# Seven-product pairs in a down projection, with operand sums and weight differences made earlier and kept in DRAM

## The chip, the cores and the metric

The kernel runs on one core of a Trainium2 chip. TensorE multiplies matrices, VectorE and ScalarE work on tiles in SBUF, GpSimd (POOL) has a few small copies and issues some DMAs, and SyncE (SP) issues nearly all loads. The metric is the device time of one execution, in microseconds.

## The reference

One decoder block on 256 tokens of width 2048, in float32: two token mixers merged into one output projection, a LayerNorm with a scaled residual, a gated MLP, a second LayerNorm, and a per-layer embedding (PLE). The part at issue:

```
def conv_gated_mlp(x, w_gate, w_up, conv_w, conv_b, w_down):
    g = causal_dwconv(x @ w_gate, conv_w, conv_b)      # width 3 along the tokens
    h = jax.nn.gelu(g) * (x @ w_up)                     # 256 x 5632
    return h @ w_down                                   # 256 x 2048

x = layer_norm(ALPHA * x + ffn, ln2_g, ln2_b)
x = x + sigmoid(x @ w_ple_gate) * (p @ w_ple_proj)
```

## The kernel before

**Precision.** Each float32 operand is split in two: a rounded part, "hi", and the remainder, "lo". A product is made of three matmuls: hi by hi, hi by lo, lo by hi. Weights are in DRAM as units (`wu[u]`) of 128 x 2048, 1 MB. A unit is loaded as two raw tiles of 128 x 1024 (512 KB) by the SP queue, into a ring of five buffers; ScalarE copies a tile to its hi (line 110), and VectorE subtracts to get the lo (line 176, or line 149 in a seven-product unit). There are six hi and six lo buffers. `prep()` (line 163) writes these steps for one unit; `unit()` writes them for up to three units ahead of the one that TensorE is given.

**Who orders the work.** The instructions of SP stand in the order in which the program text issues them. The other engines are ordered by a scheduler when the kernel is built, except for TensorE in the LayerNorm tails, which is written out by hand. Each engine then works in its order, and an instruction that waits holds up all behind it on that engine.

**The MLP.** 44 slices n of 128 hidden columns. For each, TensorE makes the gate (`psg`) and the up product (`psu`) from one unit each; VectorE and POOL do the convolution, ScalarE the GELU, and VectorE multiplies by the up part, which gives h of slice n, 128 x 256 (lines 1246 to 1282). The activations h stay in SBUF, in two forms, because of the next part.

**The down projection.** Two halves of 1024 output columns (`down`, line 1302). Each takes the 44 slices as 22 pairs; a pair needs one unit: 256 rows of the weight by 1024 columns. It is a product of 2 x 2 blocks (two token blocks of 128, two rows of the pair, two column blocks of 512). `s_half` (line 731) does a pair in one of two ways:

- classic: eight block products, 24 matmuls of 512 columns, all added in four PSUM banks. The operand is h split in hi and lo, in tiles `hC` (line 1276).
- seven products, as in Strassen's scheme: 21 matmuls. Its left operands are three blocks of h and four sums of blocks, split, in tiles `hS` (line 1270; the sums are made at line 710, on VectorE). Its right operands are three blocks of the weight and four differences of blocks. In `prep_s` (line 136) the differences are made at line 152, in place in the raw tiles, after the blocks themselves have been split; then ScalarE and VectorE split the differences. So such a unit costs VectorE four differences and holds its raw tiles longer.

The products of all the seven-product pairs of a half gather in common PSUM banks, and after the last of them `fold()` (line 771) adds them into the residual z2 by nine operations. At the end of a half `ev` (line 1308) adds the classic sums.

Eight of the 22 pairs are seven-product pairs (`DN_S`, line 55). Of these, four have their sums made in the MLP loop and four (`DN_Y`) after it. The order of the pairs (`DN_ORDER`, line 58) puts classic pairs between and behind them; in both halves the last seven-product pair, 19, is followed by more than two classic ones. Half 1 is called with tail = 2: its last two pairs, 20 and 21, are written into `end2` (line 1320) by token block, mixed with the steps of the second LayerNorm. Loads of the residual (`z2`), of LayerNorm gains and of the PLE weights are issued from within the halves.

Of the kernel before, what the change touches and what calls it, by code (L numbers as in the profile page):

```python
# [19 lines left out]
P = 128  # L20
# [32 lines left out]
WO_C = (0, 2, 4, 6, 7)  # L53


DN_S = (1, 4, 6, 9, 11, 14, 16, 19)
DN_Y = (11, 14, 16, 19)
DN_C = tuple(n for n in range(NF // 2) if n not in DN_S)
DN_ORDER = ((0, 1, 2, 4, 3, 6, 5, 9, 7, 8, 11, 10, 14, 12, 16, 13, 19, 15, 17, 18, 20, 21),
            (0, 1, 2, 4, 3, 6, 5, 9, 7, 11, 8, 14, 10, 16, 12, 19, 13, 15, 17, 18, 20, 21))  # L60
AFF1 = ((0, 2, 3), (0, 2))
AFF2 = ((0, 2), (0, 2))
LN_ORDER = (1, 0, 3, 2)
# [7 lines left out]
def tile_block(ctx: ExitStack, tc: tile.TileContext, wu, wfv, wpp, xT_in, x_in, pT_in, wlr,  # L71
# [22 lines left out]
    def s8(shape, dt=F32, name=None):  # L94
        return big.tile(shape, dt, tag="S8", name=name)
# [4 lines left out]
    def t2(name):  # L100
        return sm.tile([P, 512], F32, tag="t2", bufs=6, name=name)
# [7 lines left out]
    def copy(o, i, scale=1.0):  # L109
        return nc.scalar.activation(o, i, AF.Copy, bias=0.0, scale=scale)  # L110
# [18 lines left out]
               for nh in range(2) for i, n in enumerate(order[nh]) if n in sset[nh]}  # L129
    ready = {}  # L130

    def lo_tile(u, name):
        o = 0 if any(u in r for r in UA) else LO_SHIFT
        return rlo.tile([P, 1152], F32R, tag="lo", name=f"lo{name}")[:, o:o + 1024]

    def prep_s(u):
# [4 lines left out]
        for h, r in enumerate((r0, r1)):  # L141
            nc.sync.dma_start(r, wu[u, :, h * 1024:(h + 1) * 1024])
        b12, b11, b22, b21 = r0[:, 0:512], r0[:, 512:1024], r1[:, 0:512], r1[:, 512:1024]

        def split(src, name, e=slice(0, 1024)):
# [3 lines left out]
            nc.vector.tensor_tensor(lo, src, hi.bitcast(F32), ALU.subtract)  # L149
            return [(hi[:, o:o + 512], lo[:, o:o + 512]) for o in range(0, src.shape[1], 512)]  # L150

        sub = lambda o, a, b: nc.vector.tensor_tensor(o, a, b, ALU.subtract)  # L152
# [547 lines left out]
    def cell(o, i):  # L700

        return o[:, i, 0:P], o[:, i, P:256]
# [522 lines left out]
    hC, hS, hY, yps = {}, {}, [], {}  # L1225

    def gate_up(name):
        if first:
# [6 lines left out]
    for n in range(NF):  # L1235
        psg = gate_up(f"psg{n}")


        g = t2(f"gp{n}")
        nc.gpsimd.memset(g[:, 0:2], 0.0)  # L1240
        comb(psg, g[:, 2:258])
        cw = [chn[:, c_cw + j * NF + n:c_cw + j * NF + n + 1] for j in range(3)]
        for i in range(2):
            nc.gpsimd.tensor_copy(g[:, 258 + i:259 + i], g[:, 129 - i:130 - i])
        y = t1("yc")
        nc.vector.tensor_scalar(y, g[:, 2:258], cw[2], chn[:, c_cb + n:c_cb + n + 1],
                                ALU.mult, ALU.add)
# [8 lines left out]
        pair, j = n // 2, n % 2  # L1256
        if pair in DN_S:
            if j == 0:
                if pair in DN_Y:
                    if not hY:  # L1260
                        hY.append(s8([P, len(DN_Y), 2, 256], name="hY"))
                    yps[pair] = hY[0][:, DN_Y.index(pair)]
                else:
                    yps[pair] = t2("yp").rearrange("p (k t) -> p k t", t=S)
            nc.vector.tensor_tensor(yps[pair][:, j, :], y, u, ALU.mult)
            if j == 1 and pair not in DN_Y:
                hS[pair] = sums(yps.pop(pair), f"hS{pair}")
        else:
            nc.vector.tensor_tensor(y, y, u, ALU.mult)
            i = DN_C.index(pair)  # L1270
            if i % 2 == 0 and j == 0:
                hC[i // 2] = (s8 if i < 12 else late.tile)([P, 4, 512], F32R,
                                                           name=f"hC{i // 2}")
            dst = hC[i // 2][:, i % 2 * 2 + j, :]
            copy(dst[:, 0:256], y)
            nc.vector.tensor_tensor(dst[:, 256:512], y, dst[:, 0:256].bitcast(F32),
                                    ALU.subtract)
        if n >= 4:
            pull(1)

    for pair in DN_Y:
        hS[pair] = sums(yps.pop(pair), f"hS{pair}")


    z2 = [None, None]
# [15 lines left out]

    def down(nh, tail, mid):
        def cl(pair, j, t):
            i = DN_C.index(pair)
            a = hC[i // 2][:, i % 2 * 2 + j, :]
            return a[:, t * P:t * P + P], a[:, 256 + t * P:256 + t * P + P]

        def ev(t, c, ps):
            g = 2 * nh + c
            with tc.high_priority(P_STAT if tail else 0):  # L1310
                nc.vector.tensor_tensor(z2of(t, g), z2of(t, g), ps, ALU.add)
                if tail:
                    bn(t, g)

        s_half("dn", nh, DN_ORDER[nh], DN_S, cl, lambda pair, i: cell(hS[pair], i), z2of, ev,
               tail, mid, end2, 1 if tail else 3)

    turns = []
# [206 lines left out]
```

## Time and profile before

| | |
|---|---|
| median of 3 runs | 1666.52 us (1666.16 to 1666.75) |
| the profiled execution | 1666.29 us, its span 1664.5 us |
| TensorE busy | 1658.4 us of the span |
| VectorE busy | 1264.9 us, 76% |
| ScalarE busy | 884.0 us, 53% |
| moved by DMA | 331 MB, 199 GB/s in the mean |

The span runs from the first instruction to the last; the time of the execution has 1.8 us more around it. In the trace the MLP begins at 842.9 us, in the tail of the first LayerNorm, and ends at 1333, the first half of the down projection between 1333.8 and 1448, and the second between 1448 and 1562. In a row of groups the parts are: the line, the engine, the operation, output and inputs with their sizes, the count, then the busy time and the mean of one in ns, then the idle time of the engine just before them and what ended it. "x" on TensorE's rows counts matmul instructions. Names such as `raw`, `hi`, `lo`, `dn`, `dn_p`, `z` are those of the program's tiles; `dn_p` are the PSUM banks of the seven products, `dn` the banks of the classic sums.

### The profile page before, as it was taken

The numbers are of one execution on the slowest core, as the hardware profiler recorded it, in microseconds if no ns is written. First come the engines' busy times: TensorE is split into PE (matmuls) and PEld (weight loads), VectorE is DVE, ScalarE is ACT, GpSimd is POOL, SyncE is SP. The second block draws the span as 40 slices with busy tenths as digits, with TensorE's granted clock in tenths as the row PEclk, the third lists the DMA queues.
The fourth block names the chain that finished last, engine by engine and source line by source line (L and its number), as shares of the span: only waits on it lengthen the run. The fifth ranks groups of instructions, "written<-read, shape, count | busy, mean of one in ns | idle before, by whom it ended". The sixth has DMA issues, their size and how long they took to land.

```text
span 1664.5 us, 24153 instructions
## 1 busy us (share of the span) xinstructions
PE 1658.4 (100%) x8966; PEld 1440.9 (87%) x8966; DVE 1264.9 (76%) x1895; ACT 884.0 (53%) x1293; POOL 43.1 (3%) x171
## 2 busy tenths in 40 slices
PE   9999999999999999999999999999999999999998
PEld 8988888888888888888898888888888888888887
DVE  7776877888876757778987777766667798888874
ACT  6755555655554654545475455544444565455543
POOL 0000000000000000000010000000000000000000
PEclk9999999999999999999999999999999999999999
DMA  8755455545664555567655665555555556676554
GB/s 321 248 170 170 169 176 175 185 155 199 202 227 172 172 177 191 190 214 257 229 190 191 215 215 190 190 189 191 190 189 190 177 180 225 215 265 236 175 188 155
DMA packets 92007, 331.04 MB, mean 199 GB/s; under 512 B 10296, under 2 KB 11584, under 8 KB 90736
## 3 DMA queue, kind: packets, MB, share of 16 engines
q1 hardware_dynamic: 91104, 325.29, 57.4%
q0 software_dynamic: 784, 4.20, 0.7%
q8 instruction: 70, 1.15, 0.3%
q14 instruction: 49, 0.40, 0.1%
HBM read 324.20 MB, written 5.25 MB: 198 GB/s over the span
## 4 chain that ended last, share of the span: by engine, by line
PE 98%; DMA 0%; DVE 0%; ACT 0%; POOL 0%; issue 0%; SPq 0%; POOLq 0%
PE dn L753 11%; PE psu L243 9%; PE psg L243 9%; PE psm L243 7%; PE pg L289 5%; PE psu L245 5%; PE psg L245 5%; PE wo L753 4%; PE gv L753 4%; PE psm L245 4%; PE psa L243 4%; PE gr L289 3%; PE dn_p L753 3%; PE fv L408 2%; PE gr L753 2%; PE psa L245 2%
## 5 line engine op out<-in xcount | busy, mean ns | idle before, releaser
L176 DVE TENSOR_TENSOR lo<-raw,hi 128x1024 fp32r<-128x1024 f32 x512 | 623.2, 1222 | 298.1 <-ACT hi L110 296.7
L110 ACT ACTIVATE hi<-raw 128x1024 fp32r<-128x1024 f32 x512 | 540.2, 1059 | 507.3 <-issue 232.9
L243 PE MATMUL psu<-x1T,hi 128*128 128x512 f32 x688 | 240.4, 392 | 0.0
L243 PE MATMUL psg<-x1T,hi 128*128 128x512 f32 x672 | 234.8, 392 | 0.0
L245 PE MATMUL psu<-x1T,lo 128*128 128x256 f32 x688 | 192.3, 280 | 0.0
L245 PE MATMUL psg<-x1T,lo 128*128 128x256 f32 x672 | 187.8, 280 | 0.0
L243 PE MATMUL psm<-xT,hi 128*128 128x512 f32 x512 | 181.2, 396 | 0.0
L243 PEld LDWEIGHTS psu<-x1T,hi 128*128 128x128 f32 x688 | 129.1, 188 | 27.6
L243 PEld LDWEIGHTS psg<-x1T,hi 128*128 128x128 f32 x672 | 126.1, 188 | 27.0
L245 PE MATMUL psm<-xT,lo 128*128 128x256 f32 x512 | 143.2, 280 | 0.0
L245 PEld LDWEIGHTS psu<-x1T,lo 128*128 128x128 f32 x688 | 130.7, 190 | 0.0
L245 PEld LDWEIGHTS psg<-x1T,lo 128*128 128x128 f32 x672 | 127.6, 190 | 0.0
L753 PE MATMUL dn<-hi,hC 128*128 128x512 f32 x448 | 123.8, 389 | 0.0
L243 PEld LDWEIGHTS psm<-xT,hi 128*128 128x128 f32 x512 | 96.2, 188 | 19.7
L110 ACT ACTIVATE hi_t<-raw 128x1024 fp32r<-128x1024 f32 x56 | 59.5, 1062 | 84.4 <-DVE raw L152 69.5
L753 PEld LDWEIGHTS dn<-hi,hC 128*128 128x128 f32 x448 | 84.0, 188 | 17.4
L245 PEld LDWEIGHTS psm<-xT,lo 128*128 128x128 f32 x512 | 97.2, 190 | 0.1
L243 PE MATMUL psa<-oT,hi 128*128 128x512 f32 x256 | 89.5, 392 | 0.0
L149 DVE TENSOR_TENSOR lo_t<-raw,hi_t 128x1024 fp32r<-128x1024 f32 x56 | 68.4, 1222 | 5.2 <-ACT hi_t L110 3.6
L245 PE MATMUL psa<-oT,lo 128*128 128x256 f32 x256 | 71.6, 280 | 0.0
L753 PE MATMUL dn<-lo,hC 128*128 128x512 f32 x224 | 70.2, 389 | 0.0
L289 PE MATMUL pg<-hi,x2T 128*128 128x512 f32 (+1 forms) x256 | 69.7, 380 | 0.0
(375 smaller groups left out, 2992.6 us busy)
## 6 DMA issues: line engine op xcount, KB each, us to landing
raw<-in_wu_dram SPq DMA_DIRECT2D x568, 512.0 KB, 4.0
fvraw<-in_wfv_dram SPq DMA_DIRECT2D x13, 524.0 KB, 7.0
lnb<-in_lng_dram SPq DMA_DIRECT2D x4, 1024.0 KB, 9.5
z<-in_x_dram SPq DMA_DIRECT2D x2, 1024.0 KB, 6.8
praw<-in_wpp_dram SPq DMA_DIRECT2D x4, 512.0 KB, 5.0
x1d<-z POOLq DMA_DIRECT2D x2, 1024.0 KB, 6.2
z<-x1d SPq DMA_DIRECT2D x4, 512.0 KB, 7.5
xraw<-in_xT_dram SPq DMA_DIRECT2D x7, 256.0 KB, 6.9
```

The source lines that it names most:

```text
L110: return nc.scalar.activation(o, i, AF.Copy, bias=0.0, scale=scale)
L149: nc.vector.tensor_tensor(lo, src, hi.bitcast(F32), ALU.subtract)
L176: i = nc.vector.tensor_tensor(lo, raw, hi.bitcast(F32), ALU.subtract)
L243: nc.tensor.matmul(ps, lhsT=hi[i // 8 if hoff == 0 else 0][:, w0 % 1024:w0 % 1024 + P], rhs=a[:, kt % 4, :], start=first and i == 0, stop= ...
L245: nc.tensor.matmul(ps[:, 256:512], lhsT=lo[i // 8 if hoff == 0 else 0][:, w0 % 1024:w0 % 1024 + P], rhs=a[:, kt % 4, 0:256], start=False, ...
L289: nc.tensor.matmul(bs[j][:, 0:m], lhsT=x, rhs=v[:, o:o + m], start=first and i == 0, stop=last and i == 2)
L408: nc.tensor.matmul(fbk[t][c][:, 0:n], lhsT=x, rhs=w[:, o:o + n], start=kt == 0 and i == 0, stop=kt == 15 and i == 2)
L753: nc.tensor.matmul(ps, lhsT=x, rhs=w, start=todo[id(ps)] == total[id(ps)], stop=todo[id(ps)] == 1)
```

## The change

- 12 pairs are done by seven products instead of 8, in both halves, and the pairs run in their natural order, 0 to 21.
- The four left sums of such a pair are made in the MLP loop, split there, and stored in DRAM (`sd`, two stores of 256 KB by POOL's queue). In the down projection each seven-product unit loads its 512 KB of sums back by SP (`hS`, now per half and pair). The three operands that are plain blocks come from `hC`, which now holds all 44 slices.
- For 8 of the 12 pairs (`DN_T`), in both halves, so 16 units, the four weight differences are made during the MLP: `park_gen` loads the unit (1 MB, SP), VectorE makes the four differences in it, and POOL's queue stores it in DRAM (`td`, 1 MB). It starts at slice 6, and its steps are spread over the rest of the loop. In the down projection such a unit takes four raw tiles: the half tile b11 and the tile b22/b21 from the weight, and two tiles of differences from `td`. VectorE makes no differences there then.
- `DN_Y` and the sums after the loop are gone.

```diff
-DN_S = (1, 4, 6, 9, 11, 14, 16, 19)
-DN_Y = (11, 14, 16, 19)
...
+DN_ORDER = (tuple(range(NF // 2)),) * 2
+DN_S = (1, 2, 4, 6, 7, 9, 11, 12, 14, 16, 17, 19)
+DN_T = (2, 4, 7, 9, 12, 14, 17, 19)
...
+    parked = {dn0 + nh * (NF // 2) + n: nh * len(DN_T) + i
+              for nh in range(2) for i, n in enumerate(DN_T)}
...
+    def park_gen():
...
+        for u, i in parked.items():
+            w = s8([P, 2048], name=f"td{i}")
+            nc.sync.dma_start(w, wu[u])
+            yield
+            for h in range(2):
+                differences(w[:, 0:1024], w[:, 1024:2048], h)
+            nc.gpsimd.dma_start(td[i], w)
+            yield
...
     def prep_s(u):
...
+        rt = (r0, r1)
+        if u in parked:
+            nc.sync.dma_start(b11, wu[u, :, 512:1024])
+            nc.sync.dma_start(r1, wu[u, :, 1024:2048])
+            rt = [ring.tile([P, 1024], F32, tag="raw", bufs=5, name=f"rawt{u}_{h}")
+                  for h in range(2)]
+            for h, r in enumerate(rt):
+                nc.sync.dma_start(r, td[parked[u], :, h * 1024:(h + 1) * 1024])
+        else:
+            for h, r in enumerate((r0, r1)):
+                nc.sync.dma_start(r, wu[u, :, h * 1024:(h + 1) * 1024])
+        if dn0 <= u < dn0 + NF:
+            nh, pair = (u - dn0) // (NF // 2), (u - dn0) % (NF // 2)
+            hS[nh, pair] = s8([P, 4, 256], F32R, name=f"hS{nh}_{pair}")
+            nc.sync.dma_start(hS[nh, pair].bitcast(F32), sd[DN_S.index(pair)].rearrange(
+                "p (i n) -> p i n", i=4))
...
         x11, = split(b11, "b11", slice(512, 1024))
         x22, x21 = split(r1, "b2")
-        sub(b11, b12, b11)
-        sub(b12, b12, b22)
-        t3, t1_ = split(r0, "t13")
-        sub(b22, b22, b11)
-        sub(b21, b21, b22)
-        t2_, t4 = split(r1, "t24")
+        if u not in parked:
+            differences(r0, r1, 0)
+        t3, t1_ = split(rt[0], "t13")
+        if u not in parked:
+            differences(r0, r1, 1)
+        t2_, t4 = split(rt[1], "t24")
...
+        nc.vector.tensor_tensor(h, y, u, ALU.mult)
+        dst = hC[n // 4][:, n % 4, :]
+        copy(dst[:, 0:256], h)
+        nc.vector.tensor_tensor(dst[:, 256:512], h, dst[:, 0:256].bitcast(F32), ALU.subtract)
+        if pair in DN_S and j == 1:
+            v = s_sums(yp)
+            for i in range(2):
+                w = sm.tile([P, 2, 256], F32R, tag="t2", bufs=6, name="hs")
+                copy(w[:, :, 0:P], v[:, 2 * i:2 * i + 2])
+                nc.vector.tensor_tensor(w[:, :, P:256], v[:, 2 * i:2 * i + 2],
+                                        w[:, :, 0:P].bitcast(F32), ALU.subtract)
+                nc.gpsimd.dma_start(sd[DN_S.index(pair), :, 512 * i:512 * i + 512],
+                                    w.rearrange("p i n -> p (i n)").bitcast(F32))
...
+        def st(pair, i):
+            if i < 3:
+                return cl(pair, (0, 1, 1)[i], (0, 0, 1)[i])
+            return cell(hS[nh, pair], i - 3)
```

More of the change, by code (lines that the diff above doesn't have):

```diff
@@ L130, in tile_block @@
     ready = {}
+    parked = {dn0 + nh * (NF // 2) + n: nh * len(DN_T) + i
+              for nh in range(2) for i, n in enumerate(DN_T)}
+    td = dr.tile([len(parked), P, 2048], F32, name="td")
+    sd = dr.tile([len(DN_S), P, 1024], F32, name="sd")
+    hS = {}
     def lo_tile(u, name):
@@ L134, in lo_tile, with differences @@
         return rlo.tile([P, 1152], F32R, tag="lo", name=f"lo{name}")[:, o:o + 1024]
+    def differences(r0, r1, h):
+        b12, b11, b22, b21 = r0[:, 0:512], r0[:, 512:1024], r1[:, 0:512], r1[:, 512:1024]
+        sub = lambda o, a, b: nc.vector.tensor_tensor(o, a, b, ALU.subtract)
+        if h == 0:
+            sub(b11, b12, b11)
+            sub(b12, b12, b22)
+        else:
+            sub(b22, b22, b11)
+            sub(b21, b21, b22)
+    def park_gen():
[7 more added lines that the diff above has]
+            yield
     def prep_s(u):
@@ L1224, in tile_block @@
     late.tile([P, GAPS[2]], F32, name="gap2")
-    hC, hS, hY, yps = {}, {}, [], {}
+    hC = {}
+    parks = [park_gen()]
+    n0 = 6
     def gate_up(name):
@@ L1256, in tile_block @@
         pair, j = n // 2, n % 2
+        if n % 4 == 0:
+            hC[n // 4] = (s8 if n < 40 else late.tile)([P, 4, 512], F32R, name=f"hC{n // 4}")
         if pair in DN_S:
             if j == 0:
[L1259 to L1264, printed above, removed]
@@ L1265, in tile_block @@
-            nc.vector.tensor_tensor(yps[pair][:, j, :], y, u, ALU.mult)
-            if j == 1 and pair not in DN_Y:
-                hS[pair] = sums(yps.pop(pair), f"hS{pair}")
-        else:
[L1269 to L1277, printed above, removed]
+                yp = t2("yp").rearrange("p (k t) -> p k t", t=S)
@@ new lines, in tile_block @@
+            h = yp[:, j, :]
+        else:
+            h = y
+        nc.vector.tensor_tensor(h, y, u, ALU.mult)
[11 more added lines that the diff above has]
+                                    w.rearrange("p i n -> p (i n)").bitcast(F32))
@@ L1278, in tile_block @@
         if n >= 4:
             pull(1)
-    for pair in DN_Y:
-        hS[pair] = sums(yps.pop(pair), f"hS{pair}")
+        steps = 2 * len(parked)
+        if n >= n0 and (n - n0) * steps // (NF - 3 - n0) != (n - n0 + 1) * steps // (NF - 3 - n0):
+            pull(1, parks)
+    while parks:
+        pull(1, parks)
     z2 = [None, None]
@@ L1313, in ev @@
                     bn(t, g)
-        s_half("dn", nh, DN_ORDER[nh], DN_S, cl, lambda pair, i: cell(hS[pair], i), z2of, ev,
+        s_half("dn", nh, DN_ORDER[nh], DN_S, cl, st, z2of, ev,
                tail, mid, end2, 1 if tail else 3)
```

10 lines of the change are left out of this document (2 added, 8 removed).

## The prediction

> **What bounds the kernel now.** I read the page first, then the chain in order of time through the down projection, the engines' busy time by stage, the groups of instructions, the landing times of the weight tiles, and what the SP queue waits for.
>
> ```profile
> span 1664.5 us, 24153 instructions
> PE 1658.4 (100%) x8966; PEld 1440.9 (87%) x8966; DVE 1264.9 (76%) x1895; ACT 884.0 (53%) x1293; POOL 43.1 (3%) x171
> PEclk9999999999999999999999999999999999999999
> PE 98%; DMA 0%; DVE 0%; ACT 0%; POOL 0%; issue 0%; SPq 0%; POOLq 0%
> PE dn L753 11%; PE psu L243 9%; PE psg L243 9%; PE psm L243 7%; PE pg L289 5%; PE psu L245 5%; PE psg L245 5%; PE wo L753 4%; PE gv L753 4%; PE psm L245 4%; PE psa L243 4%; PE gr L289 3%; PE dn_p L753 3%; PE fv L408 2%; PE gr L753 2%; PE psa L245 2%
> ```
>
> TensorE is busy through the whole span, at the full clock, and 98% of the chain is its own. So a matmul less is a gain in full, and any wait of TensorE, of which there is none now, is a loss in full. The chain through the first down pairs gives the prices:
>
> ```profile
> 1333.83 5.49 PE dn L753 x24
> 1339.32 0.68 PE dn_p L753 x3
> 1340.00 1.36 PE dn L753 x6
> 1341.36 2.04 PE dn_p L753 x9
> 1343.40 6.12 PE dn L753 x27
> ```
>
> Three matmuls of 512 columns take 0.68 us, 0.2267 each. A classic pair has 24 (5.44 us). A seven-product pair has 21: rows two to four and three of the 27, 0.68 + 1.36 + 2.04 + 0.68 = 4.76 us. The stages (columns: stretch, busy us of PE, PEld, DVE, ACT, POOL, granted clock, DMA share, GB/s):
>
> ```profile
> 860.00:1320.00 460.00, 460.00 (x2661) 407.02 (x2661) 329.20 (x497) 229.76 (x333) 24.32 (x129) 1.00 0.58 197
> 1334.00:1448.00 114.00, 114.00 (x505) 94.39 (x504) 98.44 (x117) 60.89 (x68) 0.00 (x0) 1.00 0.63 212
> 1448.00:1562.00 114.00, 114.00 (x505) 94.43 (x504) 97.37 (x114) 60.39 (x65) 1.00 (x1) 1.00 0.68 233
> 1526.00:1548.00 22.00, 22.00 (x99) 18.23 (x98) 20.68 (x24) 14.43 (x16) 0.00 (x0) 1.00 0.82 285
> 1490.00:1500.00 10.00, 10.00 (x46) 8.29 (x45) 7.56 (x9) 5.58 (x6) 0.00 (x0) 1.00 1.00 398
> 20.00:25.00 5.00, 5.00 (x34) 5.00 (x33) 4.30 (x5) 3.63 (x5) 0.00 (x0) 1.00 1.04 415
> ```
>
> The first is the MLP, the next two are the halves of the down projection. There VectorE is 86% busy, the DMA engines carry 212 and 233 GB/s, and TensorE never waits.
>
> **The change, part by part.**
>
> *Matmuls.* Eight pair-halves go from classic to seven products (four pairs, two halves): 8 x 3 = 24 matmuls, the 24 that the built order has fewer on PE. 24 x 0.2267 = 5.44 us off the path. Each half then needs 12 x 4.76 + 10 x 5.44 = 111.5 us of TensorE instead of 114.2.
>
> *VectorE and ScalarE in the MLP.*
>
> ```profile
> L176 DVE TENSOR_TENSOR lo<-raw,hi 128x1024 fp32r<-128x1024 f32 x512 | 623.2, 1222 | 298.1 <-ACT hi L110 296.7
> L110 ACT ACTIVATE hi<-raw 128x1024 fp32r<-128x1024 f32 x512 | 540.2, 1059 | 507.3 <-issue 232.9 <-DMA raw<-in_wu_dram 37.0 <-PE psu L243 36.3
> L152 DVE TENSOR_TENSOR raw<-raw,raw 128x512 f32<-128x512 f32 x56 | 38.5, 688 | 1.1
> L1276 DVE TENSOR_TENSOR hC<-yc,hC 128x256 fp32r<-128x256 f32 x28 | 11.7, 418 | 0.5 <-ACT hC L110 0.5
> L710 DVE TENSOR_TENSOR sums<-yp 128x128 f32<-128x128 f32 x14 | 4.1, 291 | 0.4
> L775 DVE TENSOR_TENSOR fold<-fold,dn_p 128x512 f32<-128x512 f32 x6 | 4.1, 680 | 0.0
> ```
>
> 16 units x 4 differences x 0.69 = 44 us of VectorE come in. Sums and splits: 12 pairs x (4 x 0.291 + 2 x 0.418) = 24.0 and 16 further hC remainders x 0.418 = 6.7, against some 10 (four pairs' sums) inside the loop before: 20 more. The stage goes from 329 of 460 to 393, 85%, less than the 86% at which the down projection runs without a wait. The 10 us of sums after the loop go, at no gain, since TensorE never waited for them. POOL gets 40 DMA issues between its tap copies, at the issue times below 22 us in all, on an engine with 24 of 460.
>
> *DMA in the MLP.* 16 x (1.05 in + 1.05 out) + 12 x 0.52 out = 40 MB in about 455 us, 87 GB/s on 197: 284, below the 398 of the row above.
>
> ```profile
> L1220 POOL DMA_DIRECT2D x1d<-z x2 | 1.1, 540 | 18.1 <-DVE z L1084 18.1
> x1d<-z POOLq DMA_DIRECT2D x2, 1024.0 KB, 6.2
> ```
>
> A 1 MB store took 6.2 us; a parked unit has some 21 us before its tile is needed again. Its load stands in the SP queue ahead of the next raw tiles, and VectorE's first difference can find it 2 us late, which the two to three prepared units hide. Cost 0; without that cover 16 x 2 = 32 us.
>
> *Down projection, loads.* A half has 10 classic pairs (two raw tiles), 4 seven-product pairs as before (two tiles), 8 parked ones (four tiles, the first of half size), and 12 loads of stored sums. Bytes: 14 x 1.05 + 8 x 1.84 + 12 x 0.52 = 35.7 MB; with the two z2 loads 36.7, which is 329 GB/s over 111.5 us; in the second half, with gains and PLE weights, 40.1 MB, 360 GB/s. Before it was 212 and 233. All raw tiles go through a ring of five. A slot is held from issue to landing (L), then through ScalarE's hi and VectorE's lo. The landings, in the two halves, in 1526 to 1548 and in 1490 to 1500:
>
> ```profile
> DMA to landing us min/median/max: 3.5/5.3/10.8
> DMA to landing us min/median/max: 4.6/5.9/7.2
> DMA to landing us min/median/max: 5.7/6.4/6.6
> ```
>
> So L rises with traffic: 5.3 at some 220 GB/s, 5.9 at 285, 6.4 at 398. A plain tile holds its slot for L + 1.06 + 1.22 + about 0.4 of queueing, L + 2.7. A parked unit's four: 4L + 9.7 (the first is half). A unit with differences: about 2L + 13.5 (hi, lo, two differences, lo of the other tile, hi, lo: 6.2; for the second tile 7.3). Half 0 needs 20(L + 2.7) + 8(4L + 9.7) + 4(2L + 13.5) = 60L + 186 slot-us from five slots; half 1 with two PLE tiles 62L + 191. Before it was 44L + 184, 83 us at L 5.3 against 114: that is why nothing waits. After:
> at L 5.3: 101 us against 111.5, no wait; at 5.9: 108, just enough; at 6.4: 114 and 117.6.
> I take 5.9 in half 0 (329 GB/s is nearest the 285 row) and 6.4 in half 1 (360 is nearest the 398 row). Half 1 then runs 6.1 us over. Ends: L 5.3 costs 0, L 7.2 costs 12 and 16 us.
>
> *Stored sums right behind.* In the SP queue a unit's sums stand after its four raw tiles, and the seven products read them third, 1.36 us into the unit. Where a parked unit follows a unit with differences, its fourth raw slot comes free only when that unit's lo t13 is done, and back-to-back raw issues are 1.1 us apart:
>
> ```profile
> 1350.30 1.47 SPq L172 DMA_DIRECT2D raw<-in_wu_dram  x2
> SPq L142 <- DVE lo_t L149: 72.1, 13, 8.5
> ACT hi L110 <- PE dn L753: 13.9, 10, 1.7
> ```
>
> (Two issues of 0.33 us in 1.47; SP's waits for a slot; ScalarE waiting for TensorE to free a hi tile, which shows how far ahead the preparation is.) The sums land 1.1 + 5.9 = 7.0 us after that, and 4.76 - 2.04 + 1.36 = 4.1 us lie between TensorE's own use of t13 and of the sums. So VectorE must be 2.9 us ahead there. In half 0 it starts some 4 ahead and loses about 1 per five pairs: 1 us of waits in the last group. Ends 0 and 5 (four groups, about 1.2 each).
>
> *Order, and the tail.* The last seven-product pair is now pair 19 directly before 20 and 21. In half 1 these two are the tail, so the fold meets it. The built order of VectorE there is: z2 += p1, lo 266_0, fold += p6, lo 266_1, z2 += fold, lo 267_0, z2 += p5, lo 267_1, fold += p7, z2 += dn 00. p6 is complete 0.68 us before the tail starts. From there 0.68 + 1.22 puts lo 266_1 at 1.3 us into the tail, wanted at 0.9; then 0.69 + 1.22 and 0.68 + 1.22 put 267_0 at 3.2 and 267_1 at 5.1, wanted at 1.6 and 2.3. The last is 2.9 us late, and TensorE waits that long. Now VectorE idles there:
>
> ```profile
> 1554.24 0.69 DVE L1311 TENSOR_TENSOR z<-z,dn 128x512 f32<-128x512 f32 x1 [4.85 <-PE dn L753]
> 1562.20 1.53 PE L289 MATMUL pp<-pw,pTs 128*128 128x512 f32 x6
> 1563.56 0.60 PE L1041 MATMUL ptl<-ident,z 128*128 128x128 f32 x4
> ```
>
> The LayerNorm behind it moves by about the same, so nothing is added. Ends 0 (if TensorE had waited before, p6 and the tail move together, so 0 only if the order differed on the chip) and 5. In half 0 the same fold is covered by two classic pairs.
>
> *Sum.* -5.44 + 0 (MLP) + 1 + 6.1 + 2.9 = +4.6 us on the profiled execution's 1666.29 (span 1664.5 and 1.8 around it; 0.2 below the median): 1671 us.
>
> **A rule weighed.** The rows of five and ten microseconds carried 415 and 398 GB/s. The Trainium skill, "DMA: Bandwidth & Descriptors", Specifications, gives a limit of about 358 GB/s for a core's HBM, and says that a core alone may show more. By that limit half 1's 40.1 MB would take 112.0 us, and the sum would be 1666.3 - 5.4 + 0.5 + 2.9 = 1664.3. The two rows disagree with it as a ceiling; no row here shows 100 us at such a rate.
>
> **Rivals.**
> 1. Loads hidden, tail paid: 111.5 us is just enough at L = (557.5 - 186)/60 = 6.2 in half 0 and (557.5 - 191)/62 = 5.9 in half 1, so L is at most 5.9 in both. For it: raw landings of 3.5 when few are in flight, and the sums are extra transfers outside the ring. Against it: 5.9 already at 285 GB/s. 1666.3 - 5.4 + 2.9 = 1663.8. Chance 0.18.
> 2. The whole saving stands: as rival 1, and VectorE reaches the fold so that the tail's tiles are in time, 1660.9, faster. It decides if TensorE waits less than 2 us in all. For it: now there is no wait at VectorE's 86%. Against: the order's dependence on p6. Chance 0.15.
> 3. Both halves are bound by transfers: L 7, (420 + 186)/5 = 121.2 and (434 + 191)/5 = 125, 9.7 and 13.5 over: 1666.3 - 5.4 + 23.2 + 2.9 = 1687. For it: landings up to 10.8 beside the gain loads. Against: as TensorE waits, traffic falls. Chance 0.09.
> 4. The MLP waits: late parked loads hold VectorE, in order, and use up its 67 free us, 4 per unit. Against: the row of 197 GB/s leaves room. Some 5 us on the forecast, 1676. Chance 0.07.
> 5. The transfer engines, not the ring, bound half 1. The stage rows give 212/0.63, 233/0.68 and 285/0.82, 336 to 348 GB/s at a full share. 40.1 MB at 343 take 116.9 us, 5.4 over, the 36.7 MB of half 0 107.0, none: 1666.3 - 5.4 + 5.4 + 2.9 = 1669.2. Against: 398 at share 1.00. Chance 0.04. The rule above is the same with a smaller price.
>
> **How the numbers follow.** Forecast 0.47, its own range 1667 to 1679. About 0.2% (3.3 us) is what a measurement here can tell from no change. Faster: rival 2 and an edge of rival 1, 0.16. Same: rivals 1 and 5 and the lower end of the forecast, 0.28. Slower: the rest, 0.56. The range reaches from rival 2 up to just short of rival 3: 1661 to 1684.
>
> **What would show it.** Right: MLP with TensorE still full and VectorE near 85%; in the down projection TensorE waiting for hS loads and for lo tiles, more in half 1; landings near 6 us; the first matmuls of unit 267 waiting for lo, with some 3 us in the tail. Wrong: no waits in the halves (rival 1), landings at 7 or more (3), waits in psg or psu (4).

## The result and the profile after

The changed kernel took 1689.84 us in the median of four runs (1687.47 to 1690.69), the kernel before 1666.34: 1.0139 times as long, interval 1.0121 to 1.0156. The forecast was 1671 with a range up to 1684. The sign was right, the size was not. The profiled execution, the shortest of the four, has a span of 1685.7 us, 21.2 more than before. Three lines of the changed kernel's page (the span, the engines' busy time, and the shares of the chain of work that ended last), and its stages (columns as in the prediction; stretches: the MLP, half 0, half 1, its tail):

```profile
span 1685.7 us, 24498 instructions
PE 1663.6 (99%) x8942; PEld 1435.6 (85%) x8942; DVE 1299.2 (77%) x1975; ACT 901.4 (53%) x1325; POOL 73.0 (4%) x211
PE 83%; DMA 7%; DVE 6%; issue 2%; ACT 2%; SPq 0%; POOL 0%; POOLq 0%; ACTq 0%; DVEq 0%
```

```profile
860.00:1320.00 460.00, 460.00 (x2662) 407.02 (x2661) 373.11 (x605) 237.38 (x361) 54.23 (x168) 1.00 0.79 283
1334.00:1450.00 116.00, 112.41 (x485) 89.64 (x483) 84.36 (x88) 64.25 (x70) 0.00 (x0) 1.00 0.87 305
1450.00:1568.00 118.00, 108.56 (x452) 84.35 (x451) 88.29 (x94) 63.98 (x69) 0.00 (x0) 0.99 0.89 322
1568.00:1582.00 14.00, 11.91 (x50) 8.90 (x49) 13.18 (x21) 5.47 (x7) 1.00 (x1) 1.00 0.44 164
```

The 24 matmuls are gone (8966 to 8942). In the MLP TensorE is full and VectorE has 373 of 460 us. The time is lost in the down projection, where VectorE fell from 86% to 73 and 75%, and transfers stand on the chain. What TensorE waited for there (us in total, number of waits, the longest):

```profile
PE dn L791 <- ACT hi_t L108: 3.7, 2, 3.3
PE dn_p L791 <- ACT hi_t L108: 3.1, 3, 1.2
PE dn L791 <- DVE lo L214: 2.6, 4, 0.8
PE dn L791 <- DMA hS<-sd: 1.5, 2, 0.9
PE dn_p L791 <- DVE lo_t L188: 1.3, 3, 0.6
PE dn L791 <- DVE lo_b L188: 1.0, 2, 0.6
```

The largest are for `hi_t`, the rounded differences. Below, "waits" are what a stretch takes, from the start of its first matmul to the start of the next stretch, beyond 0.2267 us for each of its matmuls; they take in the slow starts behind a wait. By this count half 0 has 6.6 us, half 1 up to its tail 15.8, and the tail 3.0. With -5.4 for the matmuls the down projection is 19.9 us longer (248.4 against 228.5), and the stage behind it is 1.3 longer: together the 21.2. Some expectations below quote counts that differ from this one; the text gives this one throughout.

Where the waits begin is seen in SP's queue around 1500 us (start, time from the first issue to the end of the last, queue, line, tile, number of issues):

```profile
1498.23 1.33 SPq L177 DMA_DIRECT2D raw<-in_wu_dram  x2
1499.66 0.46 SPq L181 DMA_DIRECT2D hS<-sd  x1
1502.05 0.33 SPq L169 DMA_DIRECT2D raw<-in_wu_dram  x1
1504.70 0.33 SPq L170 DMA_DIRECT2D raw<-in_wu_dram  x1
1505.98 10.07 SPq L174 DMA_DIRECT2D rawt<-td  x2
1516.14 0.38 SPq L181 DMA_DIRECT2D hS<-sd  x1
```

L177 is pair 11, which makes its differences in place; L169 to L174 are the four tiles of pair 12, which is parked. Its last tile is issued ten microseconds behind the third. This is the longest of the eight such places: the in-place unit's own tiles took 11.5 us to land here, behind the two 1 MB gain loads issued at 1497, where the median of half 1 is 6.1. At the other seven the last tile came 1.3 to 8.9 us behind the third. With each tile's issue matched to its landing and to the end of its lo, the trace shows a ring that is full throughout: a slot is taken again 0.03 us after it is free, nearly everywhere. The first in-place and the first parked unit of half 0 were loaded while the MLP still ran. Without these two, parked tiles behind a classic unit were held 2.4 us after landing, the other parked tiles 5.0, and an in-place unit's own two tiles 7.0.

### The profile page after: what moved, and what is told of

Same layout as the page of the kernel before. It is cut to its first block, busy times and chain, and to the rows that moved or that the text cites. A ratio compares the mean times of both kernels' runs of the same rounds, so it can differ in the third digit from the quotient of the medians.

```text
span 1685.7 us, 24498 instructions
## 1 busy us (share of the span) xinstructions
PE 1663.6 (99%) x8942; PEld 1435.6 (85%) x8942; DVE 1299.2 (77%) x1975; ACT 901.4 (53%) x1325; POOL 73.0 (4%) x211
## 4 chain that ended last, share of the span: by engine, by line
PE 83%; DMA 7%; DVE 6%; issue 2%; ACT 2%; SPq 0%; POOL 0%; POOLq 0%; ACTq 0%; DVEq 0%
PE psu L281 9%; PE psg L281 9%; PE psm L281 7%; DMA raw<-in_wu_dram 6%; PE psu L283 5%; PE psg L283 5%; PE pg L327 5%; PE gv L791 4%; PE psm L283 4%; PE psa L281 3%; PE fv L446 3%; PE gr L327 3%; PE dn L791 2%; PE gr L791 2%; PE psa L283 2%
## 5 line engine op out<-in xcount | busy, mean ns | idle before, releaser
L214 DVE TENSOR_TENSOR lo<-raw,hi 128x1024 fp32r<-128x1024 f32 x496 | 603.7, 1221 | 239.7 <-ACT hi L108 237.6
L108 ACT ACTIVATE hi<-raw 128x1024 fp32r<-128x1024 f32 x496 | 523.1, 1058 | 443.2 <-issue 145.4
L791 PE MATMUL dn<-hi,hC 128*128 128x512 f32 x320 | 90.0, 390 | 0.0
L108 ACT ACTIVATE hi_b<-raw 128x512 fp32r<-128x512 f32 x72 | 59.9, 841 | 43.1 <-DMA raw<-in_wu_dram 22.0
L188 DVE TENSOR_TENSOR lo_b<-raw,hi_b 128x512 fp32r<-128x512 f32 x72 | 68.0, 952 | 17.0 <-ACT hi_b L108 16.8
L108 ACT ACTIVATE hi_t<-raw 128x1024 fp32r<-128x1024 f32 x40 | 42.5, 1062 | 66.9 <-DVE raw L142 49.6
L791 PEld LDWEIGHTS dn<-hi,hC 128*128 128x128 f32 x320 | 59.8, 188 | 13.0 <-ACT hi L108 0.6
```

The costliest lines, as they stand in the source:

```text
L214: i = nc.vector.tensor_tensor(lo, raw, hi.bitcast(F32), ALU.subtract)
L791: nc.tensor.matmul(ps, lhsT=x, rhs=w, start=todo[id(ps)] == total[id(ps)], stop=todo[id(ps)] == 1)
```

## The experiments

Two theories stood against each other. The ring theory: slots, not bytes, are short, because tiles that have landed wait for the in-place unit ahead of them. The bandwidth theory: the transfers themselves are the limit, since the DMA engines carry 385 to 393 GB/s in some stretches where TensorE waits (1505 to 1515, 1550 to 1556 us). Against it stand stretches with waits and far less traffic: 224 GB/s from 1545 to 1550 and 203 from 1515 to 1520.

**A sixth slot, with narrow lo tiles.**

```diff
-GAPS = (96, 64, 80)
+GAPS = (16, 16, 16)
...
-        return rlo.tile([P, 1152], F32R, tag="lo", name=f"lo{name}")[:, o:o + 1024]
+        return rlo.tile([P, 1040], F32R, tag="lo", name=f"lo{name}")[:, o:o + 1024]
...
-            raw = ring.tile([P, 1024], F32, tag="raw", bufs=5, name=f"raw{u}_{h}")
+            raw = ring.tile([P, 1024], F32, tag="raw", bufs=6, name=f"raw{u}_{h}")
```

> The changed kernel with six raw tiles in the ring instead of five; room for it comes from narrower lo tiles (1040 columns allotted instead of 1152) and smaller gaps between the pools. The ring theory: in the changed kernel every raw slot is taken again 0.03 us after it is free, all through the down projection, and the two halves hold some 590 slot-us each in 118 us. With six slots that is 98 us, less than TensorE's 111.5, so the waits of the halves (6.2 and some 15 us) go, and only the tail (2.6) stays: about 1666 us, 1662 to 1672. The bandwidth theory (the engines are full at 385 to 393 GB/s where TensorE waits): a sixth tile in flight only makes each landing longer, 6.0 us to about 7.2, and the time stays at 1685 or above.

Measured: 1689.43 us, so by its time the bandwidth theory. But the trace says otherwise: counting only gaps of more than 0.05 us, since all matmuls were slower in this run, the down projection had 10 us of waits with its tail instead of 24.5, none of them in half 0. The MLP ended 13.5 us later, with TensorE full. The run could not be read by its total, and two more runs (below) took its parts apart.

**No parked unit straight behind an in-place one.**

```diff
-DN_ORDER = (tuple(range(NF // 2)),) * 2
+DN_ORDER = ((0, 1, 3, 2, 5, 4, 6, 8, 7, 10, 9, 11, 13, 12, 15, 14, 16, 18, 17, 19, 20, 21), (0, 1, 3, 2, 5, 4, 6, 8, 7, 10, 9, 11, 13, 12, 15, 14, 16, 18, 17, 19, 20, 21))
```

> The changed kernel with the pairs of both halves in the order 0, 1, 3, 2, 5, 4, 6, 8, 7, 10, 9, 11, 13, 12, 15, 14, 16, 18, 17, 19, 20, 21, so that no parked unit comes straight behind a unit that makes its differences in place; the bytes, the matmuls and the tail are the same. The ring theory: parked tiles behind such a unit are held 5.0 us after landing, others 2.4; 28 tiles by 2.6 us less some for the classic tiles that now stand there, over five slots, is 7 to 10 us: 1679 to 1684. The bandwidth theory: the same bytes, so no change, 1687 to 1691.

Measured: 1707.16 us, 17 more than the changed kernel with the same bytes. Both expectations were wrong, and the miss says what the ring does. SP's queue behind pair 11 of half 0 in this run:

```profile
1382.51 1.61 SPq L177 DMA_DIRECT2D raw<-in_wu_dram  x2
1384.75 3.12 SPq L211 DMA_DIRECT2D raw<-in_wu_dram  x2
1389.92 0.33 SPq L169 DMA_DIRECT2D raw<-in_wu_dram  x1
1398.60 0.33 SPq L170 DMA_DIRECT2D raw<-in_wu_dram  x1
1401.70 1.46 SPq L174 DMA_DIRECT2D rawt<-td  x2
```

Two tiles of the in-place unit, two of the classic one and the first of the parked one fill the five slots. The parked unit's other three tiles are then issued only after the in-place unit is done, 8.7 us later. In the natural order it was one tile. So the theory has to count which tiles stand behind the full ring, not how long each is held in the mean.

**No parking.**

```diff
-DN_T = (2, 4, 7, 9, 12, 14, 17, 19)
+DN_T = ()
```

> The changed kernel with no unit parked: all 12 pairs of a half make their weight differences in place, so the 16 units' differences, stores and loads are gone from the MLP and the down projection; the stored sums stay. VectorE theory: a seven-product pair has 4.7 us more of VectorE than a classic one (four differences, 2.8, and 1.9 of splits), so a half needs 98 + 4 x 4.7 = 117 us of VectorE for 111.5 of TensorE; with VectorE at its full share each half is 6 to 9 us over, and the tail 3: 1676 to 1684, faster than the changed kernel, so parking as it was made costs more than it saves. Bandwidth theory: a half's bytes fall from 37 to 30 MB, 270 GB/s, no wait: 1664.

Measured: 1686.77 us, 3 less than with parking, a little above the range of the VectorE theory. The halves:

```profile
1336.00:1448.00 112.00, 108.81 (x474) 88.19 (x473) 102.54 (x117) 61.67 (x68) 0.00 (x0) 1.00 0.72 254
1448.00:1562.00 114.00, 104.50 (x429) 81.19 (x428) 104.19 (x124) 57.33 (x64) 0.00 (x0) 0.97 0.73 264
```

VectorE is at 91 to 92% and the DMA engines at 0.73, and TensorE waits nearly as much as in the changed kernel. So twelve pairs a half are too many in place, and parking took VectorE's load away and put as much back as late loads.

**The sums loaded once.**

```diff
-            hS[nh, pair] = s8([P, 4, 256], F32R, name=f"hS{nh}_{pair}")
-            nc.sync.dma_start(hS[nh, pair].bitcast(F32), sd[DN_S.index(pair)].rearrange(
-                "p (i n) -> p i n", i=4))
+            if not hS:
+                hS[0] = s8([P, 4, 256], F32R, name="hS")
+                nc.sync.dma_start(hS[0].bitcast(F32), sd[0].rearrange("p (i n) -> p i n", i=4))
+            hS[nh, pair] = hS[0]
```

> The changed kernel with the stored sums loaded once (pair 1's) and used for all pairs of both halves, which leaves out 23 loads of 512 KB and with them the right values of the other pairs' sums. These loads are not in the ring. The ring theory: landings shorten a little, 6.0 to about 5.5 us, 60 x 0.5 / 5 = 6 us per half at most, and the waits for the sums (1.5 us) go: 1676 to 1684. The bandwidth theory: 6.3 MB a half at 390 GB/s are 16 us a half, so all waits of the halves go: about 1665.

Measured: 1683.11 us, in the range of the ring theory. With 40 to 60 GB/s less in the halves (262 and 263 where the changed kernel had 308 and 319 in the same stretches) 21.9 us of waits were left in the down projection of its profiled execution, of 25.3. Bytes matter, but they are not the limit by themselves.

**The half tile out of the ring.**

```diff
-        return sm.tile([P, 256], F32, tag="t1", bufs=6, name=name)
+        return sm.tile([P, 256], F32, tag="t1", bufs=5, name=name)
...
+        if u in parked:
+            b11 = sm.tile([P, 512], F32, tag="b11", bufs=1, name=f"rawb{u}")
+            r1 = ring.tile([P, 1024], F32, tag="raw", bufs=5, name=f"raw{u}_1")
```

> The changed kernel, but the half tile b11 of a parked unit has a buffer of its own (256 KB, one), so that a parked unit takes three slots of the ring of five instead of four; one of the six small t1 buffers is given up for the room. Bytes, order and matmuls are as in the changed kernel. Held-up theory: behind a unit that makes its differences in place the ring is full of tiles that have landed and wait for it, and the parked unit's last tile is issued only when that unit is done; with three slots it is issued at once, and in six places of both halves together (of eight) TensorE's waits of 1 to 3 us go: halves with 8 instead of 22 us of waits, 1674 to 1679. If the transfers are the limit, the same bytes give 1687 to 1691.

Measured: 1674.77 us, 15 less than the changed kernel with the same bytes and order, as the refined theory had it. The same place in SP's queue:

```profile
1487.83 2.82 SPq L182 DMA_DIRECT2D raw<-in_wu_dram  x2
1490.74 0.38 SPq L186 DMA_DIRECT2D hS<-sd  x1
1491.17 0.42 SPq L174 DMA_DIRECT2D rawb<-in_wu_dram  x1
1491.71 0.38 SPq L175 DMA_DIRECT2D raw<-in_wu_dram  x1
1494.10 1.60 SPq L179 DMA_DIRECT2D rawt<-td  x2
```

The last tile goes out 1.3 us behind the third. Half 0 has no wait left. 9.3 us remain in half 1 ahead of the tail, not the 10.9 that an expectation below quotes: 3.3 mainly from 1503 us on, where the two 1 MB gain loads landed, and 6.0 from 1534 on, where the PLE weights come. The tail has 3.0 as before.

**A true sixth slot, and the narrow tiles alone.** The first, whose edit is shown, has the lo tiles as before and takes its room from one t1 and one t2 buffer; the second is the narrow run with five slots.

```diff
-GAPS = (96, 64, 80)
+GAPS = (72, 64, 80)
...
-        return sm.tile([P, 256], F32, tag="t1", bufs=6, name=name)
+        return sm.tile([P, 256], F32, tag="t1", bufs=5, name=name)
...
-        return sm.tile([P, 512], F32, tag="t2", bufs=6, name=name)
+        return sm.tile([P, 512], F32, tag="t2", bufs=5, name=name)
...
-            raw = ring.tile([P, 1024], F32, tag="raw", bufs=5, name=f"raw{u}_{h}")
+            raw = ring.tile([P, 1024], F32, tag="raw", bufs=6, name=f"raw{u}_{h}")
```

> The changed kernel with six raw tiles, with the lo tiles as wide as they were (room from one t1 and one t2 buffer and 24 columns of the first gap, which moves the hi and lo tiles by 4096 bytes). In the first run with six tiles the down projection had 8 us of waits ahead of the tail instead of 22, but TensorE's matmuls were 0.9% slower in the whole kernel, as in the narrow run with five. If the narrow lo tiles were the cause of that: the MLP ends at 1334 us again and the whole takes 1672 to 1678. If slots do not matter to the waits: 1687 or above.

> The changed kernel with five raw tiles, but the narrow lo tiles and gaps of the run with six: in that run the MLP's matmuls came 0.9% slower (0.1749 us apart in the mean instead of 0.1733) with no wait between them, 13.5 us before the down projection began. If the narrow lo tiles make TensorE slow: 1700 to 1704. If the sixth slot, which moves every later tile, does: 1687 to 1692.

Measured: 1673.40 us for the true sixth slot, which does what the half tile's own buffer did; 1705.61 for the narrow tiles. The same stretch of the MLP, first with narrow tiles and five slots, then with wide ones and six (columns as for the stages):

```profile
1100.00:1200.00 100.00, 100.00 (x573) 87.74 (x572) 80.84 (x132) 51.56 (x79) 12.74 (x36) 1.00 0.80 292
```

```profile
1100.00:1200.00 100.00, 100.00 (x579) 88.44 (x578) 81.28 (x134) 52.48 (x79) 13.08 (x37) 1.00 0.81 306
```

With no wait and the full clock in both, TensorE did 573 matmuls in 100 us instead of 579; from 900 to 1320 us they started 0.1749 us apart in the mean instead of 0.1733. So the slow matmuls of the first run came from the narrow lo tiles or the smaller gaps. Which of the two it was, was not tried.

**The tail.**

```diff
-DN_ORDER = (tuple(range(NF // 2)),) * 2
+DN_ORDER = ((0, 1, 2, 3, 4, 5, 6, 7, 8, 9, 10, 11, 12, 13, 14, 15, 16, 17, 18, 19, 20, 21), (1, 2, 3, 4, 5, 6, 7, 8, 9, 10, 11, 12, 13, 14, 15, 16, 17, 18, 19, 0, 20, 21))
```

> The changed kernel with pair 0 of half 1 moved from the first place to behind pair 19, so that a classic pair of 5.4 us stands between the last seven-product pair and the tail of the two classic pairs. The fold theory: the three waits for lo in the tail (2.6 us with their slow starts) go, and nothing else moves: 1686 to 1688, none of these waits left in the trace. If instead the late loads of units 266 and 267 held the tail, the waits stay.

Measured: 1687.20 us, 2.6 less, though the four runs (1685.56 to 1688.19) overlap with those of the changed kernel. These are the three waits of the changed kernel's tail (in brackets: TensorE's idle time before, and what ended it):

```profile
1569.88 0.50 PE L791 MATMUL dn<-lo,hC 128*128 128x512 f32 x1 [0.56 <-DVE lo L214]
1571.62 0.51 PE L791 MATMUL dn<-lo,hC 128*128 128x512 f32 x1 [0.77 <-DVE lo L214]
1573.35 0.50 PE L791 MATMUL dn<-lo,hC 128*128 128x512 f32 x1 [0.76 <-DVE lo L214]
```

By the count of waits 3.0 us in the tail became 1.6, in two places instead of three, and the 1.3 us of the stage behind went too. The expectation that nothing else moves was wrong: half 1 now begins with the in-place unit of pair 1, and 5.4 us of waits stand in its first seven pairs, where the changed kernel has 0.9. Ahead of the tail the waits grew by 1.6 us in all.

What the two late lo tiles wait for is seen in VectorE's order. In both traces it makes lo tiles and operations of the fold in turn, to the end of the fold (1566 to 1574 us in the changed kernel, 1564 to 1574 here). The run without parking has the same fold directly before the tail, but VectorE makes all four lo tiles of pairs 20 and 21 first:

```profile
1565.04 3.49 DVE L215 TENSOR_TENSOR lo<-raw,hi 128x1024 fp32r<-128x1024 f32 x3
1568.73 1.23 DVE L215 TENSOR_TENSOR lo<-raw,hi 128x1024 fp32r<-128x1024 f32 x1 [0.20 <-ACT hi L108]
1569.87 0.68 DVE L813 SCALAR_TENSOR_TENSOR z<-z,dn_p 128x512 f32<-128x512 f32 x1
```

Its tail has no wait, and the stage behind is 2.4 us longer than in the kernel before. So the tail waits for the fold's operations that stand between lo tiles in VectorE's order, not for the fold's place alone.

**The loads that only half 1 has.** First the PLE weights written one pair later, in the changed kernel; then the gain loads apart, in the run with the half tile.

```diff
-    down(1, 2, {4: lambda: load_z2(1), 8: late_loads, 14: lambda: pq.append(ple_prep(1))})
+    down(1, 2, {4: lambda: load_z2(1), 8: late_loads, 15: lambda: pq.append(ple_prep(1))})
```

> The changed kernel with the loads and splits of the PLE weights written behind pair 15 of half 1 instead of pair 14. As they were, their two ring tiles came between the in-place unit of pair 16 and the parked unit of pair 17, and the wait of 3.3 us with six slow matmuls behind it (1.3) at 1550 us lies there. Behind pair 15 they come after the parked unit. If their place in the ring is the cause: 1684 to 1686, and no wait above 1 us at that place. If the cause is the traffic of that stretch: no change, 1687 to 1691.

```diff
-        gain[1] = load_gain(1)
...
-    down(1, 2, {4: lambda: load_z2(1), 8: late_loads, 14: lambda: pq.append(ple_prep(1))})
+    down(1, 2, {4: lambda: load_z2(1), 8: late_loads, 7: lambda: load_gain2(0), 12: lambda: load_gain2(1),
+             14: lambda: pq.append(ple_prep(1))})
```

> The run with the half tile in its own buffer, with only the gain loads apart (behind pairs 7 and 12 of half 1, each ahead of a classic pair). If their burst is the cause of the waits at 1503 to 1510 us (landings of 10 to 12 us there): 3 us less, 1670.5 to 1672.5, and the waits from 1530 us on stay.

Measured: 1689.60 and 1674.08 us, neither a gain. In the first the wait at 1550 us was gone and one of 4.1 us stood at 1557, at the next pair. In the second the 3.1 us at 1503 were gone, 2.0 stood at 1522, and more from 1531 on. The lead is how far the prepared tiles are ahead of TensorE; a wait that is moved out of one place comes back at the next where it is short. So a run without these loads:

```diff
-        gain[1] = load_gain(1)
+        gain[1] = [z2[0].rearrange("p t n -> p (t n)")] * 2
...
+            if half:
+                raw = z2[0][:, k, :]
```

> The run with the half tile in its own buffer and 12 pairs in both halves, without half 1's loads of the gains and of the PLE weights: the residual tile z2 of half 0 is used in their place, so the second LayerNorm's affine step and half of the PLE projection have wrong values; the instructions of the engines stay. That run had no wait in half 0 and 10.9 us in half 1 ahead of the tail. If the 3 MB that only half 1 loads, and the two ring slots they take, make the difference: no wait in half 1 before the tail, 1663 to 1666. If half 1 runs short by its units alone (VectorE, the ring), half of the waits or more stay: 1669 to 1674.

Measured: 1666.08 us. What TensorE waited for in the whole down projection, and right behind it (`pg`):

```profile
PE dn L796 <- DVE lo L219: 1.9, 3, 0.8
PE dn_p L796 <- DVE lo_t L193: 0.8, 1, 0.8
PE pg L332 <- DVE lo L219: 0.4, 1, 0.4
```

The first and the last are the tail and its stage behind. Ahead of the tail 1.5 us of waits are left in both halves together, 1.4 of them one wait in half 0; half 1 has 0.1, of 9.3. So half 1's units run as well as half 0's, and the 3 MB of gains and PLE weights with their two ring slots are what half 1 lacked. Two runs placed them elsewhere, with the tail's order and the half tile's buffer:

The first:

```diff
-    down(1, 2, {4: lambda: load_z2(1), 8: late_loads, 14: lambda: pq.append(ple_prep(1))})
+    down(1, 2, {4: lambda: load_z2(1), 8: late_loads, 6: lambda: load_gain2(0), 11: lambda: load_gain2(1),
+             14: lambda: pq.append(ple_prep(1))})
...
+            if half:
+                if k == 0:
+                    praw = s8([P, 2, 1024], name="praw")
+                raw = praw[:, k, :]
```

The second has the places 17 and 19 for the gains and 16 for the PLE weights.

> The run with the half tile in its own buffer, and three places of its remaining waits changed, all in half 1: a classic pair (0) between pair 19 and the tail; the two 1 MB gain loads apart and each ahead of a classic pair (behind the sixth and the eleventh place of the order) instead of together ahead of an in-place pair; the PLE weights' raw tiles in a buffer outside the ring. Of 13.6 us of waits in that run 3.1 stood at the gains, 7.8 at the PLE weights and 2.8 in the tail. If these were the causes: 1661 to 1665, faster than the kernel before. If they only show where a lead that is used up elsewhere runs out, the waits move to other places: 1668 to 1674.

> All 12 pairs in both halves, the half tile in its own buffer, pair 0 of half 1 ahead of the tail, PLE raw tiles outside the ring and behind place 16, and the gain loads behind places 17 and 19 of half 1, where only classic pairs are left. The run without these loads left 1.2 us of waits ahead of the tail and 2.8 in it. If their place is what counts, not their bytes: 1661 to 1664, below the run with half 0 alone (1664.8). If they now delay the last units or the first of the next stage: 1665 to 1670.

Measured: 1670.98 and 1670.53 us, 1.0027 and 1.0022 times the kernel before. In the second the raw tiles issued between 1532 and 1542 us, together with a gain load, PLE tiles and sums, landed so late:

```profile
DMA to landing us min/median/max: 10.5/11.9/11.9
```

TensorE then waited 2.4 us and started slowly behind it: 4.2 of this run's 7.3 us ahead of the tail. The first run has 8.4 there, spread over half 1. Part of both is the price of the moved pair 0: 1.5 and 2.2 us stand in the first seven pairs of half 1, where the run with the half tile has none. Its order gave back most of the 2.8 us that it saved in the tail and behind it. With twelve pairs in both halves no place that was tried hid these loads. That it is their bytes is the likeliest reading, since both runs also took the PLE tiles out of the ring; no run here shows it by itself.

**Fewer pairs.** First ten in each half, none parked; then half 0 with twelve (eight parked, half tile apart) and half 1 with the eight pairs and the order of the kernel before; then the same with half 1's gain loads behind the 16th and the 18th place (15 and 17 in the list of half 1's side steps).

```diff
-DN_S = (1, 2, 4, 6, 7, 9, 11, 12, 14, 16, 17, 19)
-DN_T = (2, 4, 7, 9, 12, 14, 17, 19)
+DN_S = (0, 1, 3, 5, 7, 9, 11, 13, 15, 17)
+DN_T = ()
```

> Ten seven-product pairs instead of twelve (0, 1, 3, 5, 7, 9, 11, 13, 15, 17), none parked, natural order, sums stored in the MLP and loaded as in the changed kernel; two classic pairs stand between the last of them and the tail. VectorE theory: a half needs 98 + 2 x 4.7 = 107 us of it for 112.8 of TensorE, 95%; twelve in place ran at 92% with 22 us of waits. If the waits go by VectorE's load, some 5 are left: 1666.3 - 2.7 + 5 = 1668.6, range 1663.6 (no wait) to 1674. If the waits of the twelve came from the loads of sums and the order, not from VectorE: also without parking above 1674.

```diff
+DN_S1 = (1, 4, 6, 9, 11, 14, 16, 19)
...
-              for nh in range(2) for i, n in enumerate(DN_T)}
+              for nh in range(1) for i, n in enumerate(DN_T)}
```

> Half 0 as in the run with the half tile in its own buffer (12 pairs, 8 of them parked, natural order), half 1 with the eight seven-product pairs and the order of the kernel before; only half 0's eight units are parked. The same run had no wait of TensorE in half 0, so 12 matmuls less there are 2.7 us in full: 1663.8. If half 1 needs the lead that half 0 used to leave it, it waits at the gain and PLE loads as in the runs so far: 1665 to 1669.

> The run with only half 0 changed (12 pairs there, 8 in half 1), with half 1's two gain loads apart and later, behind the 16th and the 18th place of its order, where only classic pairs are left. In that run TensorE waited 4.2 us in half 1, 3.2 of it at 1507 to 1509 us, where the gains landed, and ran slowly for 3 us behind it. If the gains were the cause: these go and 1663 to 1665 are left, faster than the kernel before by 0.1 to 0.2%. If half 1 lacks the lead in any case, the wait moves: 1666 to 1668.

Measured: 1673.09 us for ten, with no wait in half 0 and 9.4 us in half 1 with its tail. 1667.58 for half 0 alone (1.0004, 0.9995 to 1.0012), with 4.8 us of waits in half 1, 4.2 of them where the gains landed and just behind. 1664.81 with the gain loads later (0.9991, 0.9983 to 1.0000): 1.6 us below the kernel before, at the edge of its interval. Its trace has 1.8 us of waits by the count, and one wait that the profile lists:

```profile
PE dn_p L798 <- DVE lo_t L195: 0.8, 1, 0.8
```

Of the versions that leave nothing out it is the only one that came out below the kernel before, by less than a third of what 24 matmuls less would give.

## Why the prediction failed

- **Matmuls**: right. 24 fewer, and in the run with half 0 alone and later gain loads 12 fewer with 1.8 us of waits shortened the down projection by 0.9 us (227.6 against 228.5), as 12 x 0.2267 = 2.7 less 1.8 says.
- **The MLP at no cost**: right. The first matmul of the down projection began at 1333.70 us, before at 1333.67. The stage carried 283 GB/s for 284 forecast; VectorE had 373 us for 393 forecast.
- **The tail, 2.9**: right. 3.0 measured, in three waits for lo tiles between which VectorE did the fold's operations, the order that the prediction had read. Another place for the fold did not end it (1.6 left), but lo tiles ahead of the fold did (0.0, in the run without parking).
- **The ring, 0 and 6.1, and the sums behind it, 1**: this step failed. The forecast summed slot times (60L + 186 in half 0) and let five slots share them freely. Its landings were right in the median, 5.8 us in half 0 and 6.1 in half 1 for 5.9 and 6.4, but not one by one: behind the gain loads they took 9.9 to 11.7. Its "L + 2.7" for a parked tile was wrong behind an in-place unit, where 5.0 us passed after landing, and so was the pooling: slots come free in order, so behind an in-place unit the ring is full of landed tiles and the tile that TensorE needs next has not been asked for. Waits of 6.6 and 15.8 us came of it and of half 1's loads, where 1 and 6.1 were forecast. By the means of the trace a half holds 20 classic tiles x 9.1 + 8 in-place x 15.0 + 32 parked x 10.0 = 622 slot-us, 124 us over five slots, for 540 forecast at 5.9. In a ring that is always full such a sum must come out at the halves' own length (118.1 and 130.3 us); what it tells is where the excess sits, and 54 of the 82 slot-us are the parked tiles, 10.0 each for 8.3 forecast. Taking eight tiles a half out of the ring brought 15 us. With that the time was 1674.8, near the forecast, but with 0 and 9.3 us of waits in the halves. The waits were for hi_t and lo tiles more than for the sums (1.5 us), which the prediction had named first.
- **Half 1 beside half 0**: the forecast put half 1's extra cost on L alone. Measured were 9.3 us in half 1 and none in half 0 with the half tile out of the ring, and 0.1 in half 1 without the gains and PLE weights. The prediction counted their bytes and slots in the sum of a half, but not that the tiles beside them land late, ahead of units with no lead.
- **The stage behind the tail**, taken as 0, cost 1.3, mostly waits for lo in the first units of the PLE gate; they went with the fold's move.
- **Rivals**: the third, loads in both halves at L 7, gave 1687 by the wrong mechanism: L was 6. The first two needed no wait in the halves, and half 0 shows that without the held-up tile they would have been right there. The MLP's (fourth) did not come about. The fifth is not borne out as it was put, since the transfer engines' share in half 1 was 0.89 and half 0 waited too; that half 1's own loads count is right.
- **The rule of the Trainium skill** ("DMA: Bandwidth & Descriptors", Specifications, 358 GB/s): the trace disagrees with it as a ceiling in short stretches, as before (393 GB/s from 1553 to 1556 us); over the 118 us of half 1 it shows 322.

## What to carry to other kernels

A ring of buffers is not a pool: count which tiles stand behind the slowest holder when it is full, and whether the next one needed has been issued. One tile less in the ring was worth as much as one slot more, and a reordering meant to help made it worse. When lead is used up, moving a transfer only moves the wait, as with twelve pairs in both halves; where some lead is left, it can pay (with eight pairs in half 1, later gain loads took 4.8 us of waits to 1.8). Otherwise take bytes away, or put the new work where the stage has room (here half 0 alone).

## What was not expected of the hardware

Behind a wait TensorE ran at half its clock for some microseconds. In the changed kernel, behind the wait of 3.3 us:

```profile
1553.13 0.80 PE L791 MATMUL dn<-hi_t,hC 128*128 128x512 f32 x1 [3.29 <-ACT hi_t L108]
1553.72 0.63 PE L791 MATMUL dn<-hi_b,hS 128*128 128x512 f32 x1
1554.15 0.63 PE L791 MATMUL dn<-lo_b,hS 128*128 128x512 f32 x1
```

```profile
1553.00:1556.00 3.00, 2.87 (x7) 2.30 (x8) 1.61 (x2) 1.32 (x3) 0.00 (x0) 0.50 1.00 393
```

The matmuls start 0.43 us apart instead of 0.227, some 1.3 us lost on top of the wait. The Trainium skill, "TensorE: Matmul & The Clock Gate", Part 1, has the clock halve after an idle window of about 3.4 us; the 3.29 us here come near it. But in the run with half 0 alone two short waits, of 1.0 and 0.8 us, did it, with TensorE busy for half of the 3.4 us before (columns as for the stages; the granted clock is the third from the end):

```profile
1505.00:1508.40 3.40, 1.71 (x7) 0.84 (x5) 2.16 (x4) 2.32 (x3) 0.00 (x0) 1.00 0.52 145
1508.50:1512.00 3.50, 3.50 (x9) 2.74 (x10) 3.50 (x4) 2.00 (x3) 0.00 (x0) 0.51 0.90 322
```

So no single wait has to fill the window; what share of it is enough, these runs do not show. And narrower lo tiles with smaller gaps between the pools, which change only where tiles lie in SBUF, made TensorE 0.9% slower with no wait shown: 13.7 us by the end of the MLP.
